# One stage of a decoder kernel: its background taps counted with a lag, projections in another order, two stores exchanged, scalings moved to ACT

## The chip, the cores and the metric

One core of one Trainium2 chip. The metric is the device time of one execution in microseconds (us). Three runs of the kernel before gave 2774.73, 2774.76 and 2777.68; the median is 2774.76.

## The reference

Three transformer blocks follow each other on 512 tokens of width 1024, all in float32. The change touches only the first block's parallel mixers: a gated delta rule with 8 heads of 128 and a causal depthwise convolution 31 taps wide, both fed by one projection.

```python
def chunk_gated_delta_rule(q, k, v, g, beta):
    ...
    m = jnp.where(strict, jnp.einsum("bhncd,bhnmd->bhncm", kb, kc) * decay, 0.0)
    t_sys = jnp.eye(CHUNK, dtype=q.dtype) + m
    u = lax.linalg.triangular_solve(t_sys, vb, ...)
    w = lax.linalg.triangular_solve(t_sys, kb * jnp.exp(gc)[..., None], ...)
    a_qk = jnp.einsum("bhncd,bhnmd->bhncm", qc, kc) * decay
    def step(state, xs):
        v_new = u_i - w_i @ state
        o_i = (q_i * exp(g_i)) @ state + a_i @ v_new
        state = state * exp(g_last) + k_dec.T @ v_new
        return state, o_i

def parallel_mixers(h, ...):
    qkv, z, a, bt, glu, gates = jnp.split(h @ w_in, offs, axis=-1)
    qkv = jax.nn.silu(causal_depthwise_conv(qkv, gdn_conv_qkv))      # 4 taps
    o = rms_norm(o, gdn_norm_g) * jax.nn.silu(z)
    c = c_lin * jax.nn.sigmoid(c_gate)
    c = causal_depthwise_conv(c, conv_dw_w) + conv_dw_b              # 31 taps
    c = jax.nn.silu(layer_norm(c, conv_ln_g, conv_ln_b))
    y = jax.nn.sigmoid(g_a) * y_a + jax.nn.sigmoid(g_c) * y_c
```

## The kernel before, in words

Every projection is computed as three float32r matmuls per block of 128 input features (the weights and the activations are each split into a high and a low part; helper `mm3`, lines 212 to 214). A weight tile is loaded by SP, rounded to its high part by ACT (line 346) and its low part is a subtraction (line 347), on POOL in the stage of the change and on DVE elsewhere.

The stage of the change ("gdn" in the code) keeps feature-major tiles of 128 x 512. Its projections come as **units**: 24 matmuls of 128x512 that fill one PSUM bank of three ("pj"), one unit for each of q, k, v of a head (`gdn_rows`), two for each of 8 slices of the convolution (`glu_conv`), one for each z of a head (`gdn_z`) and 8 gates (`gdn_gate`). Beside the units run **processes**, generators that issue a few instructions and say after how many nanoseconds of TensorE work they want to go on:

- `post` in `gdn_rows`: the 4-tap convolution of a row tile (ACT line 842, three DVE taps at line 844), Silu, transposes and norms.
- `gdn_decay`: exponentials of a head's decays (8 per pair of heads, ACT line 911), then the products kk and qk; the former goes to DRAM ("sm").
- `gdn_blocks`: the pair's diagonal blocks of 16 come back (line 938, tile ub), are inverted on DVE, and go out as Y and, transposed, as X (lines 952 and 955), and are loaded as 128x128 matrices (line 960).
- `gdn_join`: the blocks are joined to inverses of 32, 64 and 128 with matmuls between X, Y and mt, with copies on ACT (lines 993, 1003, 1013) and two DVE operations at the first level. Its steps stand JOIN_NS apart.
- `gdn_head`: the recurrence over 4 chunks, three steps per chunk, CHUNK_NS apart: r on DVE (line 1030) and the product of q with the state scaled on ACT (line 1031), v_new on ACT (line 1038), then the state on DVE (line 1047) and the output's sum (line 1052). At the end the output's norm: squares on ACT (line 1058), a power on POOL (line 371), a scaling on POOL (line 1066), four transposes and the product with z on DVE (line 1073).

The 31 taps of a slice of the convolution are **background** work: the first on ACT (line 646), 30 on DVE (line 650), into the single PSUM bank "cv".

The order is set by a planner that runs while the program is recorded (`step`, `fill_dve`, `keep_order`): a TensorE clock adds a fixed price per matmul, a due process comes first, else the next unit that may run. `fill_dve` pops taps as long as its DVE clock is behind the TensorE clock, and `keep_order` sets the DVE clock to the later of the two before it adds a price of 180 + 1.1 n ns. The engines keep this order; what is left of the taps at the end of the stage is issued then, ahead of the next stage, whose low parts are made on DVE.

After the stage come the gate projection of the convolution's branch, the split of the heads' outputs on DVE, and `conv_norm`, whose transposes (line 690) read the convolution's result.

## Time and profile before

| what | value |
|---|---|
| median of three runs | 2774.76 us |
| profiled execution: own time / span | 2774.21 us / 2772.4 us |
| busy share of the span: PE / weight loads / DVE / ACT / POOL | 96% / 78% / 49% / 38% / 16% |
| mean granted TensorE clock | 0.986 |
| matmuls | 13720 |

The span is the stretch between the first and the last instruction; the profiled execution's own time is 1.8 us longer and is within 0.6 us of the median. A matmul's recorded end is modelled, so a busy PE tells that matmuls stand close together, not that they run at their peak; what can be gained is read from PE's idle time, from what ended it, and from the granted clock.

### The profile page before, as it was taken

The page shows a single profiled execution, that of the slowest core. Times are in us where ns is not written, and L with a number is a line of the kernel's source. Part 1 is how long each engine was busy: PE and PEld are TensorE (multiplying, and loading weights), DVE is VectorE, ACT ScalarE, POOL GpSimd, SP SyncE. Part 2 cuts the span into 40 slices and gives each one's busy share as a digit, 9 for nine tenths or more (in the row PEclk, how much of TensorE's full clock was granted, in tenths as well). Part 3 has the DMA queues.
Part 4 walks back from the last instruction along what each step waited for, and adds up shares of the span by engine and source line. Part 5 has one row for each costly group of instructions (what it writes and reads, how often), then busy time and mean ns, then how long its engine had stood idle before and what let it go on. Part 6 is the DMA issues. An engine that isn't in the chain of part 4 may idle for free. (4 is left out here: it accounts for less than half of the span.)

```text
span 2772.4 us, 35041 instructions
## 1 busy us (share of the span) xinstructions
PE 2670.9 (96%) x13720; PEld 2173.4 (78%) x13720; DVE 1370.9 (49%) x2472; ACT 1064.5 (38%) x1999; POOL 445.2 (16%) x344
## 2 busy tenths in 40 slices
PE   9999999998898899999999989999999999999998
PEld 8888887777687688888888867875786767888887
DVE  3223357665568556453222375674455464632324
ACT  3322236554443333433222254563255564332221
POOL 0101115444331010001101130131002001110011
PEclk9999999999899899999999999999999999999999
DMA  5323255455445234524333234212335122532322
GB/s 190 96 99 99 93 118 90 89 78 95 61 73 90 79 127 135 172 81 160 99 99 94 96 108 123 90 43 81 98 93 91 57 58 96 172 102 99 99 92 83
DMA packets 330421, 277.32 MB, mean 100 GB/s; under 512 B 50360, under 2 KB 282512, under 8 KB 330256
## 3 DMA queue, kind: packets, MB, share of 16 engines
q1 hardware_dynamic: 292768, 251.20, 33.8%
q10 hardware_dynamic: 37488, 23.88, 2.9%
q8 instruction: 108, 1.77, 0.3%
q14 instruction: 57, 0.47, 0.1%
HBM read 256.64 MB, written 20.49 MB: 100 GB/s over the span
## 5 line engine op out<-in xcount | busy, mean ns | idle before, releaser
L347 DVE TENSOR_TENSOR wl<-wr,wh 128x1024 fp32r<-128x1024 f32 (+3 forms) x364 | 444.5, 1221 | 801.1 <-ACT wh L346 799.7
L212 PE MATMUL mm<-x,wl 128*128 128x512 f32 (+1 forms) x2112 | 812.9, 385 | 10.7 <-POOL wl L347 5.9
L214 PE MATMUL mm<-x,wh 128*128 128x512 f32 (+1 forms) x2112 | 797.9, 378 | 0.0
L213 PE MATMUL mm<-x,wh 128*128 128x512 f32 (+1 forms) x2112 | 797.8, 378 | 0.0
L346 ACT CAST wh<-wr 128x1024 fp32r<-128x1024 f32 (+3 forms) x425 | 436.3, 1027 | 811.0 <-PE mm L214 502.7
L212 PEld LDWEIGHTS mm<-x,wl 128*128 128x128 f32 x2112 | 400.4, 190 | 83.1 <-POOL wl L347 6.3
L214 PEld LDWEIGHTS mm<-x,wh 128*128 128x128 f32 x2112 | 400.1, 189 | 74.3 <-issue 1.8
L213 PEld LDWEIGHTS mm<-x,wh 128*128 128x128 f32 x2112 | 401.0, 190 | 67.2 <-issue 1.4
L347 POOL TENSOR_TENSOR h<-t,h 128x512 fp32r<-128x512 f32 x66 | 102.0, 1545 | 830.7 <-ACT h L346 830.7
L214 PE MATMUL mm<-wh,h 128*128 128x512 f32 x528 | 205.6, 389 | 0.0
L213 PE MATMUL mm<-wl,h 128*128 128x512 f32 x528 | 205.5, 389 | 0.0
L212 PE MATMUL mm<-wh,h 128*128 128x512 f32 x528 | 205.5, 389 | 0.0
L347 POOL TENSOR_TENSOR wl<-wr,wh 128x1024 fp32r<-128x1024 f32 (+1 forms) x61 | 144.2, 2364 | 297.3 <-ACT wh L346 279.1
L650 DVE SCALAR_TENSOR_TENSOR mm<-pad,cols,mm 128x512 f32<-128x512 f32 x232 | 174.8, 754 | 26.3 <-ACT mm L646 20.7
L213 PEld LDWEIGHTS mm<-wl,h 128*128 128x128 f32 x528 | 99.1, 188 | 20.6
L212 PEld LDWEIGHTS mm<-wh,h 128*128 128x128 f32 x528 | 99.1, 188 | 20.6
L214 PEld LDWEIGHTS mm<-wh,h 128*128 128x128 f32 x528 | 99.1, 188 | 20.4
L562 ACT ACTIVATE t<-mm 128x512 f32<-128x512 f32 x66 | 39.5, 599 | 127.9 <-PE mm L214 127.9
L563 DVE SCALAR_TENSOR_TENSOR t<-t,mm 128x512 f32<-128x512 f32 x66 | 45.4, 688 | 78.4 <-POOL h L347 54.9
L371 POOL TENSOR_TENSOR lr<-lr,nhalf 128x1 f32<-128x1 f32 x24 | 23.6, 984 | 371.3 <-DVE lr L370 371.3
L212 PE MATMUL mm<-m,wl 128*128 128x512 f32 (+1 forms) x224 | 81.6, 364 | 0.0
L214 PE MATMUL mm<-m,wh 128*128 128x512 f32 (+1 forms) x224 | 81.2, 363 | 0.0
(454 smaller groups left out, 3730.1 us busy)
## 6 DMA issues: line engine op xcount, KB each, us to landing
wr<-in_w_in SPq DMA_DIRECT2D x122, 512.0 KB
wr<-in_ffn_wg SPq DMA_DIRECT2D x44, 512.0 KB
wr<-in_ffn_wu SPq DMA_DIRECT2D x44, 512.0 KB
wr<-in_ffn_wd SPq DMA_DIRECT2D x44, 512.0 KB
wr<-in_w_ffn_in SPq DMA_DIRECT2D x44, 512.0 KB
wr<-in_w_ffn_out SPq DMA_DIRECT2D x22, 512.0 KB
xd<-m ACTq DMA_DIRECT2D x32, 256.0 KB
wr<-in_w_xkv SPq DMA_DIRECT2D x16, 512.0 KB
```

Of the source, the lines that this page charges most:

```text
L212: PE.matmul(o, lh[1], rh[0], start=start, stop=False)
L213: PE.matmul(o, lh[0], rh[1], start=False, stop=False)
L214: PE.matmul(o, lh[0], rh[0], start=False, stop=stop)
L346: A.copy(hi, src)
L347: (eng or V).tensor_sub(lo, src, hi.bitcast(FT))
L371: G.tensor_tensor(o, o, nhalf[:, :n], OP.pow)
L562: A.activation(sg, ps[0][f], AF.Silu)
L563: V.scalar_tensor_tensor(sg, sg, scale, ps[1][f], OP.mult, OP.mult)
L650: V.scalar_tensor_tensor(p if j < 30 else o, pad[:, j:j + T], tap31(j, c), p, OP.mult, OP.add)
```

## The change

- The planner's DVE clock may lag the TensorE clock by up to 1500 ns (DVE_LAG) before it is pulled up. JOIN_NS goes from 1700 to 2200, CHUNK_NS from 1700 to 2100.
- Units whose weights are already loaded are taken first; a unit starts only when fewer than three of the "pj" banks are held, and row tiles are taken only when fewer than three "xr" buffers are held.
- A slice's taps: its padded copy is made ahead, when fewer than 31 taps are waiting; the first tap goes from ACT to DVE.
- X is stored and loaded ahead of Y; the waits before and behind these transfers are longer.
- In a head's chunk, ACT reads the second product (q with the state) one step later, behind the wait. The head's last scaling goes from one POOL operation of 128x512 to four on ACT of 128x128.
- The list of units is in another order: z stands behind its pair of heads' rows, the convolution's slices later.

```diff
@@ module and planner
-JOIN_NS, CHUNK_NS = 1700.0, 1700.0
+JOIN_NS, CHUNK_NS, DVE_LAG = 2200.0, 2100.0, 1500.0
...
-                dve_ns[0] = max(dve_ns[0], pe_ns[0]) + 180.0 + 1.1 * n
+                dve_ns[0] = max(dve_ns[0], pe_ns[0] - DVE_LAG) + 180.0 + 1.1 * n
...
+    held = {"xr": 0, "pj": 0}
...
                 u["w"] = wload(*u["src"])
+                loaded.append(u)
...
-        if not behind:
-            u = next((u for u in units if u["may"]()), None)
+        if not behind and held["pj"] < 3:
+            u = next((u for u in loaded + units if u["may"]()), None)
@@ glu_conv
+            pad = work("pad", (128, T + 30))
+            G.memset(pad[:, :30], 0.0)
+            A.copy(pad[:, 30:], o)
             def first():
-                pad = work("pad", (128, T + 30))
-                G.memset(pad[:, :30], 0.0)
-                A.copy(pad[:, 30:], o)
-                s_.extend((pad, bank(tag="cv")))
-                A.activation(s_[1], pad[:, 0:T], AF.Identity, bias=cols["convb"][:, c:c + 1], scale=tap31(0, c))
+                s_.append(bank(tag="cv"))
+                V.tensor_scalar(s_[0], pad[:, 0:T], tap31(0, c), cols["convb"][:, c:c + 1], OP.mult, OP.add)
...
+            yield from until(lambda: len(background[1]) < 31)
+            yield from taps(o)
@@ gdn_decays
-        yield 6000.0
+        yield 11000.0
@@ post
             A.activation(x, p, AF.Copy, scale=tap(3))
+            yield 1800.0
             for d in range(1, 4):
@@ gdn_blocks
-        yield 3500.0
+        yield 7500.0
         A.dma_start(ub, blocks(gd["sm"]))
...
-        A.dma_start(blocks(gd["sy"]), yb)
         A.copy(ub, yb.rearrange("p a b -> p b a"))
         yield 1000.0
         A.dma_start(blocks(gd["sx"]), ub)
-        yield 3500.0
-        for t, s_ in (("Y", "sy"), ("X", "sx")):
+        A.dma_start(blocks(gd["sy"]), yb)
+        yield 4500.0
+        for t, s_ in (("X", "sx"), ("Y", "sy")):
...
-        yield 7000.0
+        yield 8000.0
@@ gdn_head
-            if c == 2:
+            if c == 1:
                 gd["late", h] = True
...
-                A.activation(o[:, c], p[:, 1], AF.Copy, scale=gd["egc"][:, c, h:h + 1])
+                before = p
...
             yield CHUNK_NS
+            if c:
+                A.activation(o[:, c], before[:, 1], AF.Copy, scale=gd["egc"][:, c, h:h + 1])
...
-        G.tensor_tensor(o, o, r[:, :, None].to_broadcast([128, 4, 128]), OP.mult)
+        for c in range(4):
+            A.activation(o[:, c], o[:, c], AF.Copy, scale=r[:, c:c + 1])
@@ the list of units
-            for what in (glu_conv, 0), (gdn_rows, 1), (glu_conv, 1), (gdn_rows, 2), (gdn_rows, 3), (glu_conv, 2), ...
+            for what in (glu_conv, 0), (gdn_rows, 1), (glu_conv, 1), (gdn_rows, 2), (gdn_rows, 3), (gdn_z, 0), (gdn_z, 1), ...
```

The order that comes out of it is shown at three places.

**The end of the stage, DVE.** The rows from the last product of a head with z on: before at line 1073, in the change at line 1097. Line 650 (655 in the change) is a tap, line 347 (351) with wl the low part of a weight tile, here of the next stage. Before:

```order
L1073 SCALAR_TENSOR_TENSOR ma_6612<-mm_6706,cols_292,ma_6612 128x512
L650 SCALAR_TENSOR_TENSOR ma_4988<-pad_6385,cols_306,mm_6388 128x512
L650 SCALAR_TENSOR_TENSOR mm_6735<-pad_6732,cols_299,mm_6735 128x512 x10
L347 TENSOR_TENSOR wl_6912<-wr_6910,wh_6911 128x1024
...
L347 TENSOR_TENSOR wl_7137<-wr_7135,wh_7136 128x1024
L650 SCALAR_TENSOR_TENSOR mm_6869<-pad_6866,cols_299,mm_6869 128x512
L650 SCALAR_TENSOR_TENSOR mm_6869<-pad_6866,cols_306,mm_6869 128x512 x15
L650 SCALAR_TENSOR_TENSOR ma_5924<-pad_6866,cols_306,mm_6869 128x512
```

The change:

```order
L1097 SCALAR_TENSOR_TENSOR ma_6694<-mm_6786,cols_292,ma_6694 128x512
L655 SCALAR_TENSOR_TENSOR mm_6656<-pad_6404,cols_306,mm_6656 128x512 x10
L351 TENSOR_TENSOR wl_6936<-wr_6934,wh_6935 128x1024
L655 SCALAR_TENSOR_TENSOR mm_6656<-pad_6404,cols_306,mm_6656 128x512 x4
L351 TENSOR_TENSOR wl_6966<-wr_6964,wh_6965 128x1024
L655 SCALAR_TENSOR_TENSOR ma_6157<-pad_6404,cols_306,mm_6656 128x512
```

Before, 61 taps stand behind the last product with z, the last 17 of them behind the eighth low part of the next stage; in the change there are 15 (16 with one between the two products), and the last stands behind the second low part.

**The third pair's blocks, ACT's queue.** sx and sy are the DRAM tiles of X and Y. Before:

```order
L952 DMA sy<-yb_4887 64x16x16
L953 COPY ub_4886<-yb_4887 64x256
...
L955 DMA sx<-ub_4886 64x16x16
L851 ACTIVATE xr_5224<-xr_5224 128x512
L874 COPY ma_5074<-mm_5276 128x4x128
L960 DMA Y_5287<-sy 128x4x128
L960 DMA Y_5289<-sy 128x4x128
L960 DMA X_5291<-sx 128x4x128
L960 DMA X_5293<-sx 128x4x128
```

The change:

```order
L975 DMA sx<-ub_4821 64x16x16
L976 DMA sy<-yb_4822 64x16x16
L1057 ACTIVATE t_4827<-mm_5081,gsmall_2956 128x128
L1061 ACTIVATE t_5125<-mm_5123,gsmall_2956 128x128
L866 ACTIVATE ma_4991<-xr_5067 128x4x128
L1110 ACTIVATE ma_5152<-mm_5075 128x512
L350 CAST wh_5155<-wr_5154 128x1024
L981 DMA X_5165<-sx 128x4x128
L981 DMA X_5167<-sx 128x4x128
L981 DMA Y_5169<-sy 128x4x128
L981 DMA Y_5171<-sy 128x4x128
```

X's store now stands ahead of Y's, five instructions stand between the stores and the loads where two did, and X's loads are ahead of Y's.

**The join of the third pair at the level of 32, ACT and PE.** X and Y are the two heads' matrices; line 911 (932) are the next pair's exponentials. ACT before:

```order
L1003 COPY X_5291<-mm_5460 32x4x32 x2
L874 COPY ma_5298<-mm_5474 128x4x128
L911 ACT_TABLE_LOAD
L911 ACTIVATE t_5367<-t_5367,gsmall_2956 128x128 x4
L1003 COPY X_5293<-mm_5485 32x4x32 x2
L911 ACTIVATE t_5391<-t_5391,gsmall_2956 128x128 x4
L1013 ACTIVATE Y_5287<-mm_5501 32x4x32 x2
```

ACT in the change:

```order
L1024 COPY X_5165<-mm_5370 32x4x32 x2
L932 ACT_TABLE_LOAD
L932 ACTIVATE t_5290<-t_5290,gsmall_2956 128x128 x4
L1024 COPY X_5167<-mm_5390 32x4x32 x2
L932 ACTIVATE t_5304<-t_5304,gsmall_2956 128x128 x4
L1034 ACTIVATE Y_5169<-mm_5409 32x4x32 x2
```

PE in the change (before, no matmul of 128x512 stands among these rows):

```order
L208 MATMUL mm_5370<-X_5165,mt_4771 32x32 x8
L208 MATMUL mm_5390<-X_5167,mt_4779 32x32 x8
L212 MATMUL mm_5361<-x_2468,wl_5156 128x512
L213 MATMUL mm_5361<-x_2469,wh_5155 128x512
L214 MATMUL mm_5361<-x_2468,wh_5155 128x512
L208 MATMUL mm_5409<-Y_5169,X_5165 32x32 x8
L208 MATMUL mm_5423<-Y_5171,X_5167 32x32 x8
```

The exponentials still stand among the copies of X and Y; on PE three matmuls of 128x512 now stand between the product that gives X and the one that reads it.

## Rows read from the trace of the kernel before

**Rows 1.** Busy time by stretch, PE PEld DVE ACT POOL, then clock, DMA.

```profile
388.00:898.00 510.00, 462.49 (x2600) 378.19 (x2600) 331.90 (x641) 251.03 (x586) 195.16 (x133) 0.95 0.53 85
```

**Rows 2.** PE's waits, 385 to 990 us: total, times, longest.

```profile
PE mm L690 <- DVE ma L650: 13.4, 1, 13.4
PE mm L218 <- POOL t L1066: 8.6, 4, 4.9
PE mm L208 <- DMA X<-sx: 6.9, 3, 4.2
PE mm L208 <- ACT t L1038: 6.6, 5, 4.2
PE mm L212 <- POOL wl L347: 5.9, 1, 5.9
PE mm L218 <- ACT Y L1013: 4.0, 2, 3.0
PE mm L208 <- ACT X L1003: 3.6, 4, 3.0
PE mm L208 <- ACT Y L1013: 2.8, 1, 2.8
PE mm L218 <- ACT sq L866: 2.8, 1, 2.8
```

**Rows 3.** The nine stretches of the stage at the lower granted clock, as rows 1.

```profile
432.75:436.16 3.41, 3.41 (x12) 2.72 (x11) 2.67 (x4) 2.32 (x9) 1.71 (x1) 0.50 0.16 40
518.08:524.91 6.83, 6.17 (x19) 3.98 (x20) 1.69 (x6) 4.21 (x10) 0.00 (x0) 0.50 0.02 4
589.82:600.06 10.24, 9.46 (x45) 6.81 (x45) 6.20 (x9) 6.32 (x16) 2.38 (x1) 0.50 0.10 12
634.13:640.96 6.83, 5.10 (x18) 4.52 (x19) 1.76 (x5) 0.63 (x2) 0.00 (x0) 0.50 0.27 63
681.92:685.33 3.41, 2.95 (x14) 2.95 (x15) 1.78 (x3) 0.11 (x1) 2.36 (x1) 0.50 1.03 154
695.57:709.22 13.65, 10.37 (x61) 7.48 (x61) 7.67 (x12) 7.92 (x21) 4.29 (x3) 0.50 0.00 0
757.01:763.84 6.83, 5.73 (x16) 4.67 (x17) 0.00 (x0) 0.74 (x2) 4.61 (x3) 0.50 0.58 108
845.76:849.17 3.41, 3.03 (x12) 2.31 (x10) 2.37 (x4) 0.01 (x1) 3.13 (x4) 0.50 0.14 42
900.37:917.44 17.07, 5.86 (x15) 4.71 (x16) 15.47 (x23) 3.14 (x7) 0.00 (x0) 0.50 0.05 14
sum 71.68, PE 52.08 PEld 40.14 DVE 39.60 ACT 25.40 POOL 18.48; mean PE 5.79 PEld 4.46 DVE 4.40 ACT 2.82 POOL 2.05
```

**Rows 4.** PE's timeline around the stage's end: start, duration, operation.

```profile
895.85 0.39 PE L212 MATMUL mm<-x,wl 128*128 128x512 f32 x1
896.08 0.39 PE L213 MATMUL mm<-x,wh 128*128 128x512 f32 x1
...
912.92 0.63 PE L214 MATMUL mm<-x,wh 128*128 128x512 f32 x1
913.35 0.63 PE L212 MATMUL mm<-x,wl 128*128 128x512 f32 x1
```

**Rows 5.** DVE's timeline: the last taps of the stage.

```profile
898.11 12.62 DVE L650 SCALAR_TENSOR_TENSOR mm<-pad,cols,mm 128x512 f32<-128x512 f32 x16
```

**Rows 6.** Groups of instructions by line, 385 to 915 us: busy, mean ns, idle before.

```profile
L650 DVE SCALAR_TENSOR_TENSOR mm<-pad,cols,mm 128x512 f32<-128x512 f32 x232 | 174.8, 754 | 26.3 <-ACT mm L646 20.7
L911 ACT ACTIVATE t<-t,gsmall 128x128 f32<-128x128 f32 x32 | 9.9, 388 | 0.1
L1066 POOL TENSOR_TENSOR t<-t,tiny 128x512 f32<-128x512 f32 x8 | 8.3, 1042 | 0.2
```

**Rows 7.** Waits of all engines, 385 to 912 us, as rows 2.

```profile
ACT t L1031 <- DVE t L1030: 32.6, 13, 5.7
...
DVE mm L650 <- ACT mm L646: 20.7, 8, 6.1
```

**Rows 8.** ACT's timeline: the load of ub and what follows.

```profile
634.76 0.63 ACTq L938 DMA_DIRECT2D ub<-sm  x1
635.44 0.63 ACT L1038 ACTIVATE t<-mm,gsmall 128x128 f32<-128x128 f32 x2 [5.96 <-issue]
```

More of the change, by code (lines that the diff above doesn't have):

```diff
@@ L282, in step @@
                     u["w"] = wload(*u["src"])
+                else:
+                    loaded.remove(u)
                 behind.append(u["body"](*u["w"]))
@@ L639, in taps @@
             s_ = []
+            pad = work("pad", (128, T + 30))
+            G.memset(pad[:, :30], 0.0)
+            A.copy(pad[:, 30:], o)
             def first():
-                pad = work("pad", (128, T + 30))
-                G.memset(pad[:, :30], 0.0)
-                A.copy(pad[:, 30:], o)
-                s_.extend((pad, bank(tag="cv")))
-                A.activation(s_[1], pad[:, 0:T], AF.Identity, bias=cols["convb"][:, c:c + 1], scale=tap31(0, c))
+                s_.append(bank(tag="cv"))
+                V.tensor_scalar(s_[0], pad[:, 0:T], tap31(0, c), cols["convb"][:, c:c + 1], OP.mult, OP.add)
             def tap(j):
-                pad, p = s_
+                p = s_[0]
                 V.scalar_tensor_tensor(p if j < 30 else o, pad[:, j:j + T], tap31(j, c), p, OP.mult, OP.add)
+            yield 2000.0
             background[1].append(first)
@@ L658, in consume @@
             o = cv["out"][c // 2][:, c % 2]
+            yield from until(lambda: held["xr"] < 3)
+            held["xr"] += 1
             A.copy(o, ps[0])
@@ L661, in consume @@
             A.activation(sg, ps[1], AF.Sigmoid)
+            held["pj"] -= 1 if c == 0 else 2
             yield 1500.0
             G.tensor_tensor(o, o, sg, OP.mult)
+            held["xr"] -= 1
             yield 1500.0
-            taps(o)
+            yield from until(lambda: len(background[1]) < 31)
+            yield from taps(o)
         def body(h, l):
             p = bank()
+            held["pj"] += 1
             for k in range(8):
@@ L725, in body @@
             p = bank()
+            held["pj"] += 1
             for k in range(8):
@@ L738, in gdn_decays @@
         A.copy(ab[:16], p[:16])
+        held["pj"] -= 1
         ea = tiny((128, 8))
@@ L835, in post @@
             kq, v, kdec = made()
+            yield from until(lambda: held["xr"] < 3)
+            held["xr"] += 1
             x = work("xr", (128, T))
@@ L842, in post @@
             A.activation(x, p, AF.Copy, scale=tap(3))
+            yield 1800.0
             for d in range(1, 4):
                 V.scalar_tensor_tensor(x[:, d:], p[:, :T - d], tap(3 - d), x[:, d:], OP.mult, OP.add)
+            held["pj"] -= 1
             yield 4000.0
@@ L849, in post @@
                 xf = kq[:, :, 1]
+                held["xr"] -= 1
             else:
@@ L854, in post @@
             q = four_turned(xf, 2500.0 if i == 0 else 1500.0)
+            held["xr"] -= i > 0
             if i == 2:
@@ L880, in project @@
                 p = bank()
+                held["pj"] += 1
                 for k in range(8):
@@ L978, in gdn_join @@
     def gdn_join(h):
-        mt, at, Y, X = gd["decay", h]
+        mt, at, X, Y = gd["decay", h]
         def b4(m):
@@ L1018, in gdn_head @@
         kq, v, kdec = gd["rows", h]
-        mt, at, Y, X = gd["decay", h]
+        mt, at, X, Y = gd["decay", h]
         o = t2((128, 4, 128))
@@ L2013 @@
             run(gdn_start())
+            held["pj"] = 3
             gdn_rows(0)
@@ L2016 @@
             spawn(gdn_pair(0))
-            for what in (glu_conv, 0), (gdn_rows, 1), (glu_conv, 1), (gdn_rows, 2), (gdn_rows, 3), (glu_conv, 2), \
-                    (gdn_rows, 4), (glu_conv, 3), (gdn_rows, 5), (gdn_z, 0), (gdn_z, 1), (glu_conv, 4), (gdn_rows, 6), \
-                    (gdn_rows, 7), (glu_conv, 5), (gdn_z, 2), (gdn_z, 3), (glu_conv, 6), (gdn_z, 4), (gdn_z, 5), \
-                    (glu_conv, 7), (gdn_z, 6), (gdn_z, 7), *[(gdn_gate, f) for f in range(8)]:
+            for what in (glu_conv, 0), (gdn_rows, 1), (glu_conv, 1), (gdn_rows, 2), (gdn_rows, 3), (gdn_z, 0), (gdn_z, 1), \
+                    (glu_conv, 2), (gdn_rows, 4), (gdn_rows, 5), (gdn_z, 2), (gdn_z, 3), (glu_conv, 3), (gdn_rows, 6), \
+                    (gdn_rows, 7), (glu_conv, 4), (gdn_z, 4), (gdn_z, 5), (glu_conv, 5), (gdn_z, 6), (gdn_z, 7), \
+                    (glu_conv, 6), (glu_conv, 7), *[(gdn_gate, f) for f in range(8)]:
                 what[0](what[1])
```

## The prediction

> **What bounds the kernel now.** PE is busy for 96% of the span, so time is lost where PE waits or runs at the lower of its two clock levels. The busy time by stretch comes first: in the stage of the change, 388 to 898 us, PE is busy for 462.49 of 510 us at a mean granted clock of 0.95 [rows 1], while DVE (331.90), ACT (251.03) and POOL (195.16) have room. PE's own waits say what is late [rows 2]: the nine groups shown sum to 54.6 us, and each has a releaser that the planner of this stage places. The granted clock is the third view [rows 3]: nine stretches of 71.68 us together run at 0.50, that is at 1.2 GHz in place of 2.4, and each follows one of the nine longest waits, those of 2.8 us and more in the last column of [rows 2]; the waits that were shorter are followed by none. At the lower level a matmul of 128x512 starts 0.43 us after the one before it, at the full level 0.23 us [rows 4], so of busy time at the lower level about 0.47 is lost: 0.47 x 52.08 = 24.5 us [rows 3]. With the waits that is some 79 us that lie on the path, since PE has no other cover; everything else of DVE, ACT and POOL is hidden behind matmuls.
>
> The sum is made against the profiled execution, 2774.2 us; the median of the runs shown is 0.5 us above it. About 0.2% (5.5 us) is what a measurement can tell from no change.
>
> **The change part by part.** Each term is a wait, with what its stretch at the lower clock loses (0.47 of PE's busy time there).
>
> *The end of the stage.* PE waits 13.4 us for the last tap [rows 2], and the stretch from 900.37 loses 0.47 x 5.86 = 2.8 us more [rows 3]: 16.2 us. The cause is a count: 61 taps behind the last product with z, at 12.62/16 = 0.79 us each [rows 5], are 48 us of DVE. The order of the change leaves 16 there, 12.6 us, and four gate units of 24 matmuls (4 x 24 x 0.23 = 22 us) still stand behind that product on PE; so the last tap is done before the gates are. I take -15, and keep 1 us for a DVE that runs late. Bounds: -16.2 and 0. What is late next is the low part of the next stage's first weight tile, behind 11 taps; these fit in the gates' 22 us.
>
> *A unit whose weights were not ready.* PE waits 5.9 us for one low part on POOL [rows 2], and 0.47 x 5.73 = 2.7 go with it. Three tiles were loaded ahead for other units, and this one was loaded when it began. With the list of loaded units, no unit of the changed order begins without its tile issued ahead: -8.6, bound 0 if a tile's DMA is late.
>
> *X ahead of Y.* 6.9 + 0.47 x 2.95 = 8.3 us [rows 2, 3]. The longest of the three waits is 4.2 us. X's loads now have no Y load ahead of them, and 2 us more stand between store and join. I take -6; bounds -8.3 and 0.
>
> *The load of ub.* ACT waits 5.96 us before v_new because the load of ub ahead of it waits for the store of mt [rows 8], and PE waits 4.2 us for that v_new [rows 2]; with 0.47 x 5.10 = 2.4 that is 6.6. The load now stands 4 us later: -6; bounds -6.6 and 0.
>
> *The last scaling of a head.* PE waits 8.6 us for POOL's scaling, and 1.4 go with the longest [rows 2, 3]. POOL takes 1.04 us for a head's four chunks [rows 6]; ACT does 128x128 in 0.39 [rows 6], and the first transposition can start after one of them. The power on POOL that comes first remains, so I take half, -5; bounds -10 and 0. The Trainium skill (ScalarE: Activation LUTs, Rules for kernel authors) says to put a multiplication on VectorE, not on ScalarE; no run here shows this scaling on DVE, and by that rule the sum would lose the ACT term below and be some 3 us lower.
>
> *The start.* 2.8 us for the square's copy and 0.47 x 3.41 = 1.6 [rows 2, 3]; the transposition now comes 5 us later: -3, bounds -4.4 and 0.
>
> *The joins.* The waits for X and Y on ACT, 4.0 + 3.6 + 2.8 = 10.4 us [rows 2], with the stretches from 518, 590 and 696, 0.47 x (6.17 + 9.46 + 10.37) = 12.2 [rows 3], are 22.6 us, the largest term, and the change hardly reaches it. The order shows the next pair's exponentials, eight of 0.39 us [rows 6] and a table load, still among the copies of X and Y in three of four pairs. PE has two times three matmuls more between them, 1.4 us per pair: -4; bounds -22.6 and 0.
>
> Sum of the gains: -15 - 8.6 - 6 - 6 - 5 - 3 - 4 = -47.6.
>
> *What comes in.* **DVE**: 8 first taps come from ACT, 8 x 0.75 = 6 us [rows 6], beside matmuls. More matters that the lag lets taps be issued in runs: the planner prices one at 180 + 1.1 x 512 = 743 ns where 0.79 us pass [rows 5], and lets DVE fall 1500 ns behind. r, the new state and the join's two DVE steps then queue behind taps: 7 steps per pair of heads (three r, two states, two in the join), 28 in all. Bounds: 0 (CHUNK_NS and JOIN_NS are 0.4 and 0.5 us longer, and DVE's 20.7 us of waiting for the first tap go [rows 7]) and three taps at each step, 28 x 2.36 = 66 us. I take 0.3 us per step, +8, since 0.4 us of the backlog is covered by the longer spacing and DVE was 65% busy [rows 1]. **ACT**: the four scalings stand in its queue and can wait there for r of the norm, with v_new and casts behind them: bounds +8.3 (eight heads, one POOL operation of 1.04 us each [rows 6]) and -2.4 (the short waits for v_new, 6.6 - 4.2 [rows 2], go, because ACT no longer stands 32.6 us behind r [rows 7]). I take +3.
> The longer spacing makes a pair's chain 8 x 0.5 + 12 x 0.4 = 8.8 us longer; units cover it, and as many gate units as before stand behind the last head. Without that cover the last pair alone would cost 8.8 us. The bank and buffer counts and the order of the units move work only among units that PE does anyway: nothing, with the same cover. All later stages keep their work.
>
> Sum: -47.6 + 8 + 3 = -36.6, so 2774.2 - 36.6 = **2738 us**.
>
> **The rivals.**
> *DVE becomes the queue that all wait in* (slower). If taps stand three deep (1500 ns of lag are two, the loop adds one) in front of each of the 28 steps, the DVE term is 66 in place of 8: 2774.2 - 47.6 + 3 + 66 = 2796 us. It decides from (47.6 - 3)/28 = 1.6 us per step, two taps, at which the time is 2774 again. For it speaks that the change issues more taps per stretch; against it DVE's third of free time [rows 1], and that each wait of PE lets DVE catch up. The Trainium skill (Perfetto Trace Analysis, Tensor Engine Instruction) says that ACT, DVE and GPSIMD are strict FIFOs. By that rule nothing lets r pass a tap; the trace agrees in ACT's 5.96 us behind one load [rows 8].
> *ACT becomes the queue* : the head's scaling, the start and the joins give nothing back, the X term only 4, and the new ACT cost is at its bound: -15 - 8.6 - 4 - 6 + 8 + 8.3 = -17.3, 2757 us. For it: eight exponentials and a table load still stand in the joins; against it: ACT's 32.6 us behind r go.
> *Nothing new comes in*: DVE and ACT cost 0, each term is at its bound and the joins, broken into waits too short for the clock to fall, give 8: -16.2 - 8.6 - 8.3 - 6.6 - 10 - 4.4 - 8 = -62, 2712 us.
>
> **How the numbers follow.** Forecast (2722 to 2750) 0.55; nothing new (about 2712) 0.17; ACT (about 2757) 0.17; DVE with two taps, within 0.2%, 0.04; DVE with more 0.07. The range 2708 to 2764 holds the first three with a little of each left out. Faster 0.55 + 0.17 + 0.17 = 0.89, same 0.04, slower 0.07.
>
> **What would show it.** Right: no wait of conv_norm's transposes for a tap; none of over 2 us for a low part on POOL; X waits under 2 us; v_new behind no load; joins still with waits for X and Y and lower-clock stretches behind them; few short PE waits on DVE. Wrong: many waits of PE on r or the state behind taps (DVE), ACT idle in front of the scalings (ACT), or lower-clock stretches of over 50 us in sum; then the time is above 2750.

## The result, and the profile after

The changed kernel takes 2790.91 us (median of 5 runs, 2789.83 to 2791.98); the kernel before took 2774.76 us beside it. The ratio is 1.0062 with a 95% interval of 1.0049 to 1.0075: it is **slower by about 16 us**. The forecast was 2738 us, faster, with 0.07 on slower. The profiled execution took 1.8 us more than its span, as before.

The page of the changed kernel: its span, and busy time with shares of the span.

```profile
span 2790.2 us, 35075 instructions
...
PE 2683.9 (96%) x13720; PEld 2177.7 (78%) x13720; DVE 1384.3 (50%) x2480; ACT 1063.7 (38%) x2020; POOL 437.1 (16%) x336
```

The number of matmuls is the same, 13720, so the two kernels can be laid side by side by counting them. I call **the body** the 2590 matmuls of the stage from the 1810th of the program to the 9320th before its end, and **the rest** all that follows it, the stage's end first. In the kernel before the body took 507.7 us (385.7 to 893.4) and the rest 1879.1; in the changed one the body took 540.4 us (385.8 to 926.2) and the rest 1863.9. Each of these numbers is from one profiled execution. So the end of the stage gave back 15.2 us, as forecast, and the body lost **32.7 us** where the other terms of the forecast together made a gain of some 22.

Busy time by stretch of the changed kernel, columns as in [rows 1]: first the stage, then three of its thirteen stretches at the lower clock and the sum of all thirteen, which answers to [rows 3].

```profile
388.00:931.00 543.00, 479.16 (x2597) 385.40 (x2598) 362.16 (x674) 255.22 (x616) 186.97 (x125) 0.93 0.50 81
...
606.96:624.03 17.07, 16.34 (x60) 11.52 (x61) 0.94 (x2) 6.11 (x14) 2.48 (x2) 0.50 0.51 32
...
678.64:685.47 6.83, 5.01 (x14) 4.16 (x15) 5.24 (x12) 5.56 (x23) 4.67 (x5) 0.50 0.39 117
...
794.70:801.52 6.82, 3.84 (x17) 3.87 (x18) 2.52 (x5) 2.09 (x4) 5.92 (x3) 0.50 0.73 169
...
sum 78.49, PE 68.75 PEld 53.43 DVE 38.07 ACT 28.71 POOL 28.26; mean PE 5.29 PEld 4.11 DVE 2.93 ACT 2.21 POOL 2.17
```

Without the stretch at the stage's end [rows 3], which is gone, the body had 52.08 - 5.86 = 46.2 us of PE's busy time at the lower clock; it now has 68.75. At the forecast's 0.47 that is 10.6 us more lost. PE's idle time in the body rose from 48.0 to 64.1 us, 16.1 more. These two make 26.7 of the 32.7. The other 6 are in PE's busy time too, which rose by 16.5 us in the body (459.7 to 476.3); no row tells why.

PE's waits in the changed kernel, 385 to 1000 us, as [rows 2].

```profile
PE mm L208 <- ACT t L1057: 10.5, 6, 4.2
PE mm L218 <- ACT t L846: 8.4, 2, 6.5
PE mm L208 <- DMA X<-sx: 7.0, 1, 7.0
PE mm L208 <- DVE t L1051: 6.7, 3, 4.3
PE mm L208 <- ACT X L1024: 5.4, 3, 2.2
PE mm L218 <- ACT t L1090: 4.7, 3, 3.1
PE mm L208 <- ACT t L1061: 4.0, 1, 4.0
PE mm L218 <- ACT vk L876: 3.7, 1, 3.7
...
PE mm L208 <- DVE gsmall L882: 1.6, 1, 1.6
...
PE mm L212 <- DVE wl L351: 1.3, 1, 1.3
```

Gone are the 13.4 us for the last tap and the 5.9 us for a low part on POOL [rows 2]. What has grown is ACT: its groups of 1 us and more sum to 45.5 us, against 23.3 before. The wait for X has stayed (7.0 for 6.9), now in one piece. DVE's groups sum to 10.2 us, against 3.2 beside the last tap.

Waits of all engines in the changed kernel, 385 to 930 us, and groups of instructions there by line. They answer to [rows 7] and [rows 6].

```profile
ACT pad L647 <- POOL ma L672: 16.4, 6, 3.8
ACT pad L647 <- DVE ma L655: 14.7, 2, 8.7
...
ACT t L1090 <- DVE tiny L1088: 8.3, 3, 3.4
...
ACT t L1057 <- DVE t L1051: 5.3, 4, 2.5
```

```profile
L655 DVE SCALAR_TENSOR_TENSOR mm<-pad,cols,mm 128x512 f32<-128x512 f32 x232 | 175.0, 754 | 6.4
...
L1090 ACT ACTIVATE t<-t,tiny 128x128 f32<-128x128 f32 x32 | 10.1, 391 | 8.3 <-DVE tiny L1088 8.3
```

ACT's 32.6 us of standing behind r [rows 7] have fallen to 5.3, as the later reading was to do, and DVE's 20.7 us in front of the first tap are gone. In their place ACT now stands in front of the copy into pad (31.1 us, behind POOL's product and behind taps) and of the new scaling. A tap still takes 754 ns; the 16 that stood at the stage's end [rows 5] now run in the body.

Two places show how ACT's standing reaches PE. The first is ACT's timeline in the changed kernel where the third pair's loads of X and Y meet the norm of the pair before (start, duration, operation, idle before and its releaser; ACTq is a transfer that ACT issues), and PE's beside it.

```profile
664.08 0.69 ACTq L976 DMA_DIRECT2D sy<-yb  x1
...
670.44 0.94 ACTq L981 DMA_DIRECT2D X<-sx  x2
674.41 2.41 ACTq L981 DMA_DIRECT2D Y<-sy  x2
676.86 0.31 ACT L1081 ACTIVATE t<-t 128x128 f32<-128x128 f32 x1 [6.57 <-issue]
...
679.21 0.25 ACT L846 ACTIVATE t<-mm 128x128 f32<-128x128 f32 x1
```

```profile
680.46 0.87 PE L218 MATMUL mm<-ident,sq 128*128 128x128 f32 x3 [6.50 <-ACT t L846]
```

The loads of Y stand in ACT's queue: the first waits until 674.4 for Y's store to land, 10.3 us after that store was issued, and the second is out only at 676.8. So eight squares of the norm (L1081) and the squares PE needs (L846) come 6.57 us late, and PE waits 6.50 us. This is the pattern of [rows 8], which the change removed for ub, at another load. The second place lies near the end of the body.

```profile
829.99 0.62 ACT L647 COPY pad<-ma 128x512 f32<-128x512 f32 x1 [8.72 <-DVE ma L655]
830.51 0.59 ACT L1125 ACTIVATE ma<-mm 128x512 f32<-128x512 f32 x1
831.00 1.03 ACT L350 CAST wh<-wr 128x1024 fp32r<-128x1024 f32 x1
831.93 0.63 ACT L1061 ACTIVATE t<-mm,gsmall 128x128 f32<-128x128 f32 x2
...
844.72 1.04 ACT L350 CAST wh<-wr 128x1024 fp32r<-128x1024 f32 x1 [4.86 <-DMA wr<-in_w_in]
845.67 0.36 ACT L1057 ACTIVATE t<-mm,gsmall 128x128 f32<-128x128 f32 x1
```

```profile
832.36 0.80 PE L208 MATMUL mm<-t,vk 128*128 128x128 f32 x2 [3.98 <-ACT t L1061]
...
846.08 0.80 PE L208 MATMUL mm<-t,Y 128*128 128x128 f32 x2 [4.18 <-ACT t L1057]
```

ACT stands 8.72 us in front of the pad copy, which needs a buffer that the last tap of an earlier slice still reads; a gate, a cast and v_new (L1061) stand behind it, and PE waits 3.98 us for that v_new. Then ACT stands 4.86 us in front of a cast whose weights have not landed, with the scaling L1057 behind it, and PE waits 4.18 us. From matmul 2200 to 2400 of the body (counted from its start) the changed kernel takes 56.8 us; the kernel before takes 44.0.

### The profile page after: what moved, and what is told of

It reads as the page before. It is cut to its first block, busy times and chain, and to the rows that moved or that the text cites. A ratio compares the mean times of both kernels' runs of the same rounds, so it can differ in the third digit from the quotient of the medians.

```text
span 2790.2 us, 35075 instructions
## 1 busy us (share of the span) xinstructions
PE 2683.9 (96%) x13720; PEld 2177.7 (78%) x13720; DVE 1384.3 (50%) x2480; ACT 1063.7 (38%) x2020; POOL 437.1 (16%) x336
```

## The experiments

The theory after the result was that the lag is the price: taps placed in runs stand on DVE ahead of the chains. The first rival was a single other part of the change (the pad copy, the later reading, the scaling on ACT, the spacings); the second, which came up later, was the order of instructions as a whole. For each kernel the table gives the median, the ratio to the kernel before measured beside it, and, from its profiled execution, the body, PE's idle time in it, the time of its matmuls at the lower clock (each counted to the start of the next, so 46.9 and 69.6 where the stretches gave 46.2 and 68.75), and the rest. The profiled executions lie within 4.2 us of their medians, but for lag_100_only, whose profiled execution (2773.06) is 8.5 us above its median. One kernel's own executions spread by up to 16 us (the kernel before: 2767.4 to 2783.9 over all its runs), so a few us between two bodies, each from a single execution, show nothing by themselves.

| kernel | median us | ratio, 95% | body | idle | lower clock | rest |
|---|---|---|---|---|---|---|
| before | 2774.76 | | 507.7 | 48.0 | 46.9 | 1879.1 |
| the change | 2790.91 | 1.0062 [1.0049, 1.0075] | 540.4 | 64.1 | 69.6 | 1863.9 |
| lag_only | 2802.99 | 1.0109 [1.0088, 1.0130] | 550.8 | 72.2 | 83.5 | 1865.4 |
| lag_100_only | 2764.53 | 0.9971 [0.9957, 0.9986] | 521.6 | 56.8 | 57.3 | 1863.7 |
| late_lag | 2773.07 | 1.0000 [0.9990, 1.0010] | 507.9 | 46.9 | 48.4 | 1879.0 |
| spacing_only | 2787.44 | 1.0056 [1.0041, 1.0071] | 513.1 | 52.4 | 41.5 | 1887.1 |
| undo_pad | 2790.23 | 1.0059 [1.0043, 1.0074] | 541.4 | 65.3 | 70.2 | 1864.2 |
| undo_defer | 2784.24 | 1.0034 [1.0019, 1.0049] | 531.6 | 62.4 | 57.2 | 1864.1 |
| undo_scale | 2795.01 | 1.0074 [1.0059, 1.0089] | 544.9 | 70.1 | 68.4 | 1864.1 |
| lag_900 | 2786.07 | 1.0048 [1.0034, 1.0062] | 533.7 | 66.0 | 49.6 | 1864.3 |
| lag_500 | 2773.20 | 1.0000 [0.9990, 1.0011] | 521.7 | 54.1 | 56.1 | 1864.8 |
| lag_500_headnow | 2774.61 | 1.0004 [0.9992, 1.0015] | 521.0 | 55.4 | 49.5 | 1864.3 |
| lag_500_close | 2773.09 | 1.0001 [0.9991, 1.0010] | 519.9 | 49.6 | 58.9 | 1864.8 |
| thin_before | 2757.78 | 0.9952 [0.9933, 0.9970] | 504.8 | 46.8 | 41.3 | 1864.9 |
| thin_lag_only | 2792.45 | 1.0070 [1.0053, 1.0088] | 534.3 | 65.4 | 60.3 | 1865.6 |
| thin_lag_500 | 2769.64 | 0.9985 [0.9974, 0.9996] | 519.8 | 52.5 | 58.8 | 1865.6 |
| thin_after | 2784.53 | 1.0041 [1.0026, 1.0056] | 531.1 | 64.5 | 50.6 | 1864.5 |
| nudged_spacing | 2773.25 | 0.9991 [0.9976, 1.0006] | 522.7 | 49.6 | 64.7 | 1865.8 |
| before_mix | 2763.08 | 0.9969 [0.9958, 0.9981] | 505.5 | 48.0 | 36.8 | 1871.6 |
| mix_act_scale | 2771.73 | 0.9995 [0.9986, 1.0004] | 512.6 | 52.5 | 42.7 | 1870.7 |

### The lag by itself

**lag_only** puts the lag of 1500, and nothing else, into the kernel before.

```diff
-JOIN_NS, CHUNK_NS = 1700.0, 1700.0
+JOIN_NS, CHUNK_NS, DVE_LAG = 1700.0, 1700.0, 1500.0
...
-                dve_ns[0] = max(dve_ns[0], pe_ns[0]) + 180.0 + 1.1 * n
+                dve_ns[0] = max(dve_ns[0], pe_ns[0] - DVE_LAG) + 180.0 + 1.1 * n
```

> The kernel before with one part of the change alone: the planner's DVE clock may lag 1500 ns (JOIN_NS and CHUNK_NS stay 1700). Theory ACT (what the change lost lies in new instructions that stand at the head of ACT's queue and wait): the wait of 13.4 us for the last tap goes and the rest stays, about 2758 to 2763 us, no wait of over 2 us behind line 690. Theory DVE (taps issued in runs delay r, the state and the join's DVE steps): the tail is gained too, but PE's waits on DVE in the stage rise from under 1 us to 15 or more, with clock losses: 2775 us or more.

It is 28 us slower. The rest falls to 1865.4, so the lag does clear the end of the stage, and the body rises by 43.1 us. The waits of all engines in lag_only, 385 to 940 us, show ACT behind DVE and PE behind ACT:

```profile
ACT t L1031 <- DVE t L1030: 43.5, 19, 5.6
...
ACT X L993 <- DVE mm L650: 17.0, 1, 17.0
ACT xr L851 <- DVE xr L844: 13.3, 5, 5.1
...
PE mm L208 <- ACT t L1038: 9.0, 6, 4.8
```

In the kernel before the first of these was 32.6 us [rows 7]. I read this then as the theory borne out; the thin kernels below show that it is so for less than a third.

**late_lag** applies the lag only once the last pair of heads is done, to have its gain at the end without its price.

```diff
-                dve_ns[0] = max(dve_ns[0], pe_ns[0]) + 180.0 + 1.1 * n
+                dve_ns[0] = max(dve_ns[0], pe_ns[0] - (1500.0 if ("done", 6) in gd and ("done", 7) in gd else 0.0)) + 180.0 + 1.1 * n
```

> The kernel before, with the lag of 1500 ns allowed only once the last pair of heads is done. Theory RUNS (a run of taps costs only where r, the states, the joins and ACT stand behind DVE): the body of the stage keeps its time, the wait for the last tap falls from 13.4 us to 2 to 7 us, 2764 to 2771 us. Theory ORDER (any edit of the planner reshuffles the stage and scatters its time by 10 us or more, whatever it does): the body changes too, 2765 to 2790 us.

Nothing moved: body 507.9, rest 1879.0, and PE's wait for the last tap is still 12.6 us. The trace shows why: the instructions of every engine stand in the same order, row for row, as in the kernel before. By then it is too late to place the taps.

**lag_100_only** is lag_only with 100 in place of 1500.

> The kernel before with a lag of 100 in place of 1500, everything else as before. Its matmuls stand in another order over about as many rows as with 1500 (2951 lines of difference against 3059). If the price goes by the lag's size: 2768 to 2778 us, body of the stage within 6 us of 507.7. If any such reordering costs: 2785 us or more, body 525 or more.

A lag of 100 also clears the end (rest 1863.7), and its median is 9 us under the kernel before beside it (2773.68), below what either theory expected; the body of 521.6 is above what the theory of the size expected, but comes from a profiled execution 8.5 us above that median. It does not settle "any reordering costs": the traces, which name tiles without their buffer numbers, do not bear out its premise of as many rows. There the order differs from the kernel before in 168 rows on PE and 78 on ACT, against 514 and 241 for lag_only. The smaller lag also reorders less, and this run does not separate the two.

### One part of the change undone

**undo_pad** puts the copy into pad back into the list of background work.

```diff
-            pad = work("pad", (128, T + 30))
-            G.memset(pad[:, :30], 0.0)
-            A.copy(pad[:, 30:], o)
-
             def first():
-                s_.append(bank(tag="cv"))
+                pad = work("pad", (128, T + 30))
+                G.memset(pad[:, :30], 0.0)
+                A.copy(pad[:, 30:], o)
+                s_.extend((pad, bank(tag="cv")))
...
-            yield 2000.0
...
-            yield from until(lambda: len(background[1]) < 31)
-            yield from taps(o)
+            taps(o)
```

> The changed kernel with the padded copy made again when the first tap is popped (the first tap stays on DVE). Theory ACT: the 31 us in which ACT stood at the padded copy (16.4 behind POOL's product, 14.7 behind the tap before) go, and PE's waits on ACT fall by some 10 us: 2775 to 2782 us. Theory DVE: no change, 2788 to 2793 us.

No change (body 541.4). The 3.98 us behind the pad copy go, but PE then waits 4.99 us for r on DVE near the same place: undoing one cause of a late chain uncovers the next.

**undo_defer** scales a chunk's second product at once, as before the change.

```diff
-                before = p
+                A.activation(o[:, c], p[:, 1], AF.Copy, scale=gd["egc"][:, c, h:h + 1])
...
-            if c:
-                A.activation(o[:, c], before[:, 1], AF.Copy, scale=gd["egc"][:, c, h:h + 1])
```

> The changed kernel with ACT's scaling of a chunk's second product read at once again, not a step later. Theory ACT in the form that the deferred reading holds a PSUM bank: PE's 10.5 us behind line 1057 go with three low-clock stretches, 2776 to 2782 us. Theory DVE: ACT now stands behind r again, which is late behind taps: 2791 us or slower.

6.7 us less than the change, by the medians; one of its six runs (2790.85) is as slow as the change. PE's 10.5 us behind the scaling L1057 are gone, while its waits for v_new rise from 4.0 to 8.5 us. PE's order is that of the change, row for row.

**undo_scale** puts the last scaling of a head back on POOL.

```diff
-        for c in range(4):
-            A.activation(o[:, c], o[:, c], AF.Copy, scale=r[:, c:c + 1])
+        G.tensor_tensor(o, o, r[:, :, None].to_broadcast([128, 4, 128]), OP.mult)
```

> The changed kernel with a head's last scaling on POOL again. Theory ACT: ACT's 8.3 us before the scalings go, PE's 4.7 us behind them turn into waits on POOL of about the same size: 2786 to 2790 us. Theory DVE: 2789 to 2793 us, no change.

4.1 us more than the change: the runs of the two kernels do not overlap, though the intervals of their ratios do. In this order of instructions, which stays the same on PE row for row, the scaling on ACT is worth about what the forecast took for it (5).

**spacing_only** puts only the longer spacings into the kernel before.

```diff
-JOIN_NS, CHUNK_NS = 1700.0, 1700.0
+JOIN_NS, CHUNK_NS = 2200.0, 2100.0
```

> The kernel before with JOIN_NS 2200 and CHUNK_NS 2100 alone. Theory RUNS: the short waits for v_new, X and Y shrink by some 5 us, and the chain's 8.8 us per pair are covered by units: 2766 to 2772 us. Rival: the longer chains leave fewer units for the last pair and the cover is gone there: 2778 to 2785 us.

It is 14 us slower against the kernel before beside it (2773.08), and most of that is at the end of the stage: the body rises by 5.4, the rest by 8.0. PE's waits of this kernel, 385 to 1000 us:

```profile
PE mm L690 <- DVE ma L650: 20.4, 1, 20.4
```

That wait was 13.4 [rows 2]. The last product with z runs 3.7 us later (851.3 for 847.6), and 64 taps stand behind it, for 61. In the change the lag clears this; so alone the spacings cost what they do not cost beside a lag, as lag_500_close shows next.

### The size of the lag within the change

**lag_500** and **lag_900** change one number of the change; **lag_500_headnow** adds the edit of undo_defer to lag_500, and **lag_500_close** the old spacings.

```diff
-JOIN_NS, CHUNK_NS, DVE_LAG = 2200.0, 2100.0, 1500.0
+JOIN_NS, CHUNK_NS, DVE_LAG = 2200.0, 2100.0, 500.0
```

> The changed kernel with a lag of 500 ns in place of 1500. Theory RUNS: fewer taps stand in front of a head's steps, so PE's waits on DVE and on what ACT does behind DVE fall by about half: 2772 to 2784 us, even if some taps are left at the end. Theory ORDER: 2785 to 2797 us, with no relation to the lag.

> The change with the lag at 900 in place of 1500; nothing else differs. If the lag's size is what costs the body of the stage (1500 gave 2790, 500 gave 2773), the time lies between them: 2777 to 2786 us, with the wait of the short convolution at the stage's end still gone and TensorE's body of the stage between 522 and 540 us. If 500 was only a lucky order of instructions and the lag's size says nothing, 900 may come out anywhere, as high as 2790 or more or below 2773.

> The change with the lag at 500 and a chunk's second product scaled at once, as before the change. Undoing the later reading alone gave 6.7 us with the lag at 1500, and the lag at 500 alone 18. If the two costs are separate: 2766 to 2768 us, ratio to the kernel before 0.997. If the later reading only cost because the lag had left ACT behind VectorE, 2773 as with the lag at 500 alone.

> The change with the lag at 500 and the spacings of the joins and chunks at 1700 again. In the kernel before, the longer spacings alone cost 14 us, about half of it at the end of the stage, where the change has no wait left. If the spacings cost in the body of the stage: 2765 to 2768 us. If they cost only by what they leave for the end, and the lag clears that: 2771 to 2775. If the longer spacings are needed so that the matrix unit does not wait for r and for the joins' copies beside a lagging VectorE: 2778 or more.

500, 900 and 1500 give 2773.20, 2786.07 and 2790.91: in order of size, as the theory of the lag had it, though the intervals of 900 and 1500 overlap. The rest is 1864 to 1865 in all of them, so the smallest lag keeps the whole gain at the end. But the parts do not add. The later reading, worth 6.7 us at a lag of 1500, is worth nothing at 500 (2774.61), and the spacings, 14 us by themselves, are worth nothing there (2773.09). Costs that vanish beside another setting are not costs of the part; this raised the question what the body's 32.7 us are.

### Taps that take no time

Four kernels keep the order of instructions of the kernel before, of lag_only, of lag_500 and of the change (but for a few dozen rows at the stage's end in three of them, none in lag_only), and cut a tap's duration: 20 of 512 columns, while the planner is still charged for 512. They leave most of the convolution out.

```diff
                 n = math.prod(k for _, k in inst.outs[0].ap[1:])
+                n = 512 if n == 20 else n
...
-                V.scalar_tensor_tensor(p if j < 30 else o, pad[:, j:j + T], tap31(j, c), p, OP.mult, OP.add)
+                V.scalar_tensor_tensor((p if j < 30 else o)[:, :20], pad[:, j:j + 20], tap31(j, c), p[:, :20], OP.mult, OP.add)
```

> The kernel before with every tap of the short convolution after a chunk's first cut to 20 of 512 columns (most of that convolution is left out); the order of instructions and the planner's account are those of the full taps. Both theories: the wait for the last taps at the stage's end (13.4 us) goes, so 2755 to 2762 us. If the taps' time hardly hindered the body of the stage there, the body stays at 500 to 508 us; if it did, it falls to 490 or less.

> The kernel before with the lag of 1500 alone, taps cut to 20 of 512 columns in the same way (most of the convolution left out). Body of the stage with full taps: 550.8 us. Theory that VectorE's taps stand ahead of the chains: the body falls to that of the thin kernel before, within 8 us, and the whole to 2755 to 2768. Theory that another part of the order costs: the body stays above 535 us and the whole above 2785.

> The change with the lag at 500, taps cut to 20 of 512 columns (most of the convolution left out). Body with full taps: 521.7 us. Taps' time as the cause: body 500 to 508 us, whole 2752 to 2760. Order as the cause: body 516 to 522 us, whole 2767 to 2773.

> The change with taps cut to 20 of 512 columns (most of the convolution left out). Body with full taps: 540.4 us. Taps' time as the cause: the body falls to 500 to 512 us and the whole to 2750 to 2764, level with the thin kernel before. Order as the cause (ACT's copies of the taps' input, the spacings, the later reading, buffers): the body stays at 525 us or more and the whole at 2775 or more.

These are the runs that decided. In thin_before the end of the stage is free (rest 1864.9) and the body stays at 504.8: in the kernel before, the taps cost the body some 3 us at most. In thin_lag_only the body is still 29.5 us above that (534.3), so of the lag's 43.1 us with full taps 29.5 remain without the taps' time; nothing but the order differs between these two. In thin_after 26.3 of the change's 32.7 remain (531.1 less 504.8). The medians less the rests say much the same: 34 of 42 us remain, and 27 of 31. **The taps' time on DVE accounts for some 6 us of the change's loss; some 26 are not the taps' time.** In the change these 26 are the order together with its other parts (copies and scalings on ACT, spacings, waits, limits), which thin_after does not separate. With taps that take almost no time, PE still waits for ACT in thin_lag_only (PE's waits, 385 to 930 us):

```profile
PE mm L209 <- ACT t L1039: 11.3, 8, 4.1
PE mm L219 <- ACT ma L849: 7.9, 2, 4.7
PE mm L219 <- ACT Y L1014: 7.2, 2, 3.6
```

The groups shown sum to 26.4 us; in thin_before v_new (L1039) had 7.0, this group of Y 4.0 and ma no group of its own.

### The same change, 60 ns apart

**nudged_spacing** shortens the change's two spacings by 60 ns each; every part of the change is in it.

```diff
-JOIN_NS, CHUNK_NS, DVE_LAG = 2200.0, 2100.0, 1500.0
+JOIN_NS, CHUNK_NS, DVE_LAG = 2140.0, 2040.0, 1500.0
```

> The change with its two spacings 60 ns shorter (2140 and 2040), lag 1500. It changes the order of the matmuls over about half as many rows and none of the parts. If the loss belongs to the lag and the other parts: 2784 to 2796 us as the change, body 534 to 547. If the loss is scatter of the order: the body may fall by 15 us or more, to 2775 or less, or rise as much.

2773.25 us: the time is that of the kernel before again, with the change's lag of 1500 and all its parts in place. The body is 522.7 and PE's idle time in it 49.6 us, 14.5 less. So 17.7 us of the body's loss hang on 60 ns of spacing; the other 15.0 remain, and are made up by the end of the stage (13.3). Laid beside each other by matmuls, the two are within 1.9 us of each other at every 200th up to the 1400th of the body; at the 1600th the nudged kernel is 12.3 us ahead, and 18.0 at the 2400th. The first of these is the place shown above, the loads of X and Y of the third pair. ACT's timeline of nudged_spacing there:

```profile
665.25 0.38 ACTq L981 DMA_DIRECT2D X<-sx  x1
...
666.78 0.56 ACTq L981 DMA_DIRECT2D Y<-sy  x1
...
668.42 0.31 ACT L1081 ACTIVATE t<-t 128x128 f32<-128x128 f32 x1
```

The loads are spread between the squares, each goes out in about half a microsecond, Y's store has landed when ACT comes to Y's loads, 6.8 us after the store's issue, and the squares of the norm follow 1.1 us after the last load's issue, without an idle time of their own. Where the change had 6.50 us of PE's waiting for L846, and 6.83 us at the lower clock behind it, no wait of over 2 us is left at this place. At the second place the pad copy still stands 7.72 us behind a tap, and PE waits 3.0 for v_new, but the 4.18 behind the cast are gone. The wait for X of the fourth pair has stayed (7.4 us).

### Parts of the change in the kernel before

**before_mix** takes from the change what removes a wait and leaves its chains' timing alone: loaded units first, the load of ub 4 us later, X stored and loaded ahead of Y, and the lag at the end alone, as in late_lag, where it did nothing.

```diff
+                loaded.append(u)
...
-            u = next((u for u in units if u["may"]()), None)
+            u = next((u for u in loaded + units if u["may"]()), None)
...
-        yield 3500.0
+        yield 7500.0
...
-        for t, s_ in (("Y", "sy"), ("X", "sx")):
+        for t, s_ in (("X", "sx"), ("Y", "sy")):
```

> The kernel before with the parts of the change that don't load DVE: loaded units first, the load of ub 4 us later, X stored and loaded ahead of Y with the longer waits around them, and the lag only once the last pair is done. Theory RUNS: the terms of these parts come in as predicted, 8.6 + 6 + 6 us and some 8 us at the end: 2745 to 2755 us. Theory ORDER: the waits named go, others come in their place: 2762 to 2785 us.

2763.08 us, faster than both kernels by a ratio of 0.9969 to the kernel before, though less than expected. Its PE waits, 385 to 1000 us, no longer name a transfer of X or a low part on POOL. But the body is 505.5, only 2.2 us shorter; 7.5 of the gain lie in the rest, where 53 taps in place of 61 stand behind the last product with z. In the body other waits have come in place of those removed: 12.0 us for Y on ACT, 6.8 before. The wait for the last tap and that for v_new are down to:

```profile
PE mm L693 <- DVE ma L653: 3.8, 1, 3.8
...
PE mm L208 <- ACT t L1041: 2.9, 4, 1.5
```

**mix_act_scale** adds the scaling on ACT (the edit of undo_scale, the other way round) to before_mix.

> The kernel before with loaded units first, ub loaded later, X before Y, the lag only at the end (which gave 2763 to a 2773 before) and with the last scaling of a head on ACT as four instructions. Undoing that scaling in the change cost 4 us; GpSimd's scaling ends 8.6 us of TensorE's waits in the kernel without it. If that holds here: 2756 to 2760 us, ratio 0.994 to 0.9955. If ACT has become the queue that all wait in: 2763 or more.

It is 8.7 us slower than before_mix by the medians (7 by the ratios), where the same edit gained 4.1 us within the change. PE's order is the same but for two rows. ACT stands 13.4 us in front of the four scalings here (8.3 in the change), and of the 8.6 us that PE waited for POOL's scaling in before_mix 5.1 remain, now behind ACT; a wait of 5.6 us behind a tap is new. The Trainium skill (ScalarE: Activation LUTs, Rules for kernel authors) would put this multiplication on VectorE; no run here shows it there, and between ACT and POOL the two runs differ in sign.

## Why the prediction was wrong, point by point

- **The end of the stage, -15: right.** The rest fell by 15.2 us. The cause given was right too: every kernel whose lag holds throughout, or whose taps are cut short, has a rest of 1864 to 1866. It does not take a lag of 1500: in the kernel before, 100 does it.
- **The unit without ready weights, -8.6: right** as a wait (5.9 us on POOL gone, PE's waits for low parts on DVE 1.3 us).
- **X ahead of Y, -6: failed.** 7.0 us of waiting remain. ACT came late to the issue: it stood 3.76 us behind POOL in front of the pad copy at 788.76, and the loads stood behind that. This explains at most 3.8 of the 7.0 us; PE starts 8.9 us after the issue, where the term had counted on 2 us more between store and join. In before_mix, where X and Y were exchanged and no pad copy stands ahead of the loads, the wait is gone.
- **The load of ub, -6: the wait went, and came back at another load.** 6.57 us of ACT's standing in front of the squares, 6.50 us of PE's, at 680.
- **The last scaling, -5: right here** (4.1 by undo_scale), but not a price of the edit: it cost 8.7 us when added to before_mix.
- **The start, -3, and the joins, -4: not borne out.** PE's first waits of the stage are now for vk (3.7) and L846, and PE still waits 8.3 us for X and Y on ACT (10.4 before); the stretches at the lower clock behind these waits, from 528, 607 and 703, lose 0.47 x 27.1 = 12.8 us (12.2 before).
- **DVE, +8: about right in size.** PE's waits on DVE rose by 7 us, and the taps' time is 6.4 us of the loss (32.7 less 26.3). The count behind the term was off: the trace has 56 of these steps (24 r, 16 states, 16 in the joins), seven per head and not per pair. The rival that DVE becomes the queue that all wait in, to which the forecast gave its chance of slower, is not what happened: thin_lag_only and thin_after are slow without the taps' time. That its 2796 us lie near the measured 2790.91 is coincidence.
- **ACT, +3 (-2.4 to +8.3): this is the step that failed.** PE's waits on ACT rose by 22 us, of which 4.7 came over from POOL with the scaling. The lower clock took 10.6 us more; eleven of its thirteen stretches in the body go with waits on ACT, five of eight before. The forecast's own sign of being wrong, lower-clock stretches of over 50 us in sum, came true (78.49). The bounds were taken from two known rows, the POOL operation ahead of the scaling and the short waits for v_new; what was left out is that a planner with another clock for DVE places everything anew, so that a load, a cast or a copy that waits may land in ACT's queue ahead of any of the chain's steps. The rival for ACT had the mechanism but took its price from the scalings alone (2757 us).
- **"The longer spacing costs nothing, with the same cover": right beside a lag, wrong alone** (spacing_only, 14 us).

Behind the failed step stands a larger one: the sum treated the order of instructions as given, with terms of 3 to 9 us to be added. Two orders of the same change, 60 ns of spacing apart, differ by 17.7 us, and the same edit was worth -4.1 and +8.7 us. The sum of the small terms, -36.6 + 15 = -21.6 us without the end, is hardly larger than that scatter, and the range (2708 to 2764) left it out. That the measured time lies above it by 27 us and not by 9 is itself an accident of the order.

What stays open: whether a larger lag costs more on the average of many orders. The lags 500, 900 and 1500 in the change, and 100 against 1500 alone, came out in that order; but nudged_spacing, at 1500, is as fast as lag_500, so five points do not separate size from luck. The 15.0 us that the body of nudged_spacing keeps are not attributed either: the list of units in its other order, the limits on banks and buffers and the longer waits were not undone one by one in the change. The lag of 100 together with before_mix was not tried.

## What to carry to other kernels

Where a planner writes the order of all engines from modelled clocks, change its constants by a few per cent first and measure the scatter of the time; a sum of terms smaller than that scatter forecasts nothing. Read the new order at each step that PE waits for, and look at what stands ahead of it in its engine's queue and waits there (a load's issue, a cast of weights not yet landed, a copy into a buffer in use): in these traces each of them became a wait of PE. To tell an engine's load from the order that it is given, keep the order and cut the duration of its instructions.

## What the runs showed of the hardware

**Small DVE operations stretch beside POOL.** DVE's timeline of the changed kernel around 568 us, and POOL's:

```profile
567.08 0.18 DVE L968 TENSOR_TENSOR yb<-yb,tb 64x28 f32<-64x28 f32 x1
567.55 0.35 DVE L1051 SCALAR_TENSOR_TENSOR t<-mm,gsmall,vk 128x128 f32<-128x128 f32 x1 [0.29 <-PE mm L208]
567.82 2.27 DVE L966 TENSOR_TENSOR tb<-ub,yb 64x15 f32<-64x15 f32 x1
570.12 2.31 DVE L968 TENSOR_TENSOR yb<-yb,tb 64x15 f32<-64x15 f32 x1
```

```profile
567.67 4.74 POOL L351 TENSOR_TENSOR wl<-wr,wh 128x1024 fp32r<-128x1024 f32 x2 [3.69 <-ACT wh L350]
```

An operation on 64x15 took 2.27 us where one on 64x28 had taken 0.18; each of the two ends within 0.1 us of the end of one of POOL's two operations of 2.37 us, and PE waited 4.32 us for the r behind them (a tap and the three taps of a row tile stand between). The Trainium skill (SBUF — State Buffer, Who interferes with whom) says that a DVE instruction with two SBUF inputs contends with a GpSimd instruction that reads SBUF, over ports that are an exclusive lock; the trace agrees, 2.27 us for 0.18. Nineteen operations of DVE in the stage of the change lie more than 0.4 us above their group's median, by 27.0 us in all (nineteen before, 17.6 us); all but one of them, and all nineteen before, end within 0.1 us of the end of a POOL operation.

**A long stretch at the lower clock without a long wait.** The forecast read from [rows 2, 3] that only waits of 2.8 us and more are followed by the lower clock. PE's timeline of the changed kernel at 607 us:

```profile
607.69 0.63 PE L218 MATMUL mm<-ident,Y 64*64 64x64 f32 x4 [1.27 <-ACT Y L1034]
608.25 0.79 PE L212 MATMUL mm<-x,wl 128*128 128x512 f32 x1
608.84 0.63 PE L213 MATMUL mm<-x,wh 128*128 128x512 f32 x1
609.26 0.63 PE L214 MATMUL mm<-x,wh 128*128 128x512 f32 x1
```

The waits ahead were 2.03 us (to 604.80) and 1.27 us (to 607.69), and the clock stayed at 0.50, 1.2 GHz, for 17.07 us with PE busy for 16.34 of them. PE ran a join's small matmuls there, 64x64, with three or six wide ones between them. In five of the thirteen stretches no wait of 2.8 us stands in front or within; the longest there are 1.87 us (before 507.98), 1.43 (528.46), 2.03 (606.97), 2.25 (702.54) and 1.39 (767.39), while waits of 1.70 and 1.59 us at 559.5 and 562.9 were followed by none. So the length of one wait does not decide. Breaking a join's waits into shorter ones, on which the third rival counted, did not keep the clock up.
